# A transformer block in one core: two more tiles by seven products, and part of the low halves on GpSimd

## The chip, the core and the metric

The kernel runs on one core of a Trainium2 chip. The time is the device time of one execution, in microseconds, as the median of several runs. Five engines matter: TensorE (PE in the profile) for matrix products, with its weight loads shown apart (PEld), VectorE (DVE), ScalarE (ACT), GpSimd (POOL), and SyncE (SP), which here only issues transfers.

## The reference: what is computed

One layer of an encoder on 256 tokens of width 2048, all in float32. The first half is an RMS norm, a combined input projection, windowed attention beside a Fourier mix, and an output projection added to x. The second half, where most of the time and most of the change lie, is a feed-forward block with a gate of 5504 channels (43 tiles of 128):

```python
def _conv_ffn(h, w_up, dw_w, dw_b, w_down):
    up = h @ w_up
    gate, val = up[..., :D_FF], up[..., D_FF:]
    gate = conv_width_3(gate, dw_w) + dw_b      # depthwise, along the tokens
    act = jax.nn.gelu(gate, approximate=False) * val
    return act @ w_down

x = x + jnp.concatenate([a, f], axis=-1) @ w_out
x = x + _conv_ffn(_rmsnorm(x, norm2_g), w_up, dw_w, dw_b, w_down)
return _rmsnorm(x, normf_g)
```

(The convolution is written short here.)

## The kernel before: tiles, stages and order

**Split products.** TensorE multiplies in a rounded float32 format (fp32r). To keep accuracy, each weight tile is split into a high part, its rounding, which ScalarE makes (`split_high`, L190, with its operation at L197), and a low part, the rest, which VectorE makes by a subtraction (`split_low`, L199, at L205). Activations are split in the same way, and a product is the sum of three: high by high, high by low, low by high. A weight tile comes as a *unit* of 128 x 2048 values (1 MB) into one of three `raw` buffers by a load on SP's queue; `split(i)` makes the two parts in three rotating buffers each, and once the low part is made, `load(i + 3)` is issued into the raw buffer that came free.

**Feed-forward.** Up units, one for the gate and one for the value of each of the 43 tiles, are still weights: 16 blocks of 128 x 128, each with a matmul of 512 columns for the high part and one of 256 for the low part (L372). Behind them come small steps: `scaled_sum` (L1011) adds the two halves of the sum (ScalarE copies one out, L1013; VectorE adds, L1015) and multiplies by `r2b`, the row of 1/rms (L1016); `gate_conv` (L1019) is the convolution, one operation of ScalarE and two of VectorE; `gate_gelu`; `val_mult`.

**Down projection by seven products.** For most tiles, the down projection works on 2 x 2 blocks: two halves of a group's tiles, two halves of the tokens, and pairs of 512 output columns. Instead of eight block products there are seven, of sums of blocks (a scheme of the Strassen kind). `GROUPS` (L81) names the groups: (first tile, tiles per half). In the kernel before these are tiles 0 to 35: a group of 2 + 2 and four of 4 + 4. Each group is multiplied for two values of c (pairs of columns), so 14 products, named P1, P7, N5, N3, P6, P2, N4. A product with n tiles per half takes 3n matmuls of 512 columns. Its weights are read from a ring of two buffers `rawd` (`ring_load`, on SP's queue) and from `sumw`, a running sum of weight blocks: `first_sums` (L1140) makes the first sum on VectorE, the others are accumulating transfers issued by GpSimd (L1134, L1136, L1145). `split_product` (L1117) splits them (L1129, L1130). The operands are sums of activation blocks, made by `operand` and `operand_sums`. When the last value tile of a group is ready, these steps are spread over the next seven items (`up_posts`).

**The rest.** Tiles in `LATE` (36 to 39) are multiplied directly, as four "down" units of 2048 columns (L355 to L357); tiles in `LAST` (40 to 42) as four "last" units at the very end (L1410 to L1412). Each result is added to x by VectorE (`product_out`, `shared_out`, `down_out`, `last_post`). `first_squares` to `scaled` are the final norm.

**Order.** Nothing is scheduled automatically: each engine runs its instructions in the order in which the program emits them. `ff_items` (L101) writes out the order of the feed-forward: `PATTERNS` (L89) says for each group how up units (u), products (s) and down units (d) follow each other, `"uuu" + "su" * 13 + "s"` for the first four. In step n the matmuls of item n are emitted, then the posts put `beside` it, then the split of item n + 2, then the posts put `behind` it (`ff_step`, L1160). So a split is emitted two items ahead of its matmuls.

**Before the feed-forward**, the output projection works through 16 units with `unit(i, work)`: its matmuls, the steps put beside, the split of unit i + 2, the steps put behind. For each of four column blocks of x, `flip_x_out` turns the block (a transposition on VectorE and four transfers on SP's queue), `flip_x_in` reads it back. For the last block, `last_out_post` (L1298) does that by hand among the first up units, and makes `r2b`: the sum of squares, a power on GpSimd (L309), and a way out to memory and back as a row (`row_out`, L320; `row_in`).

Of the kernel before, what the change touches and what calls it, by code (L numbers as in the profile page):

```python
# [11 lines left out]
ALU = mybir.AluOpType  # L12
# [65 lines left out]
OUT_ORDER += [(c, k) for c in (2, 3) for k in range(4)]  # L78


GROUPS = [(0, 2), (4, 4), (12, 4), (20, 4), (28, 4)]  # L81
LATE = list(range(36, 40))
LAST = list(range(40, NF))
PRODUCTS = [
    ["P1", "P7", "N5", "N3", "P6", "P2", "N4"], ["P1", "N5", "P7", "N3", "P6", "P2", "N4"]
# [1 line left out]


PATTERNS = ["uuu" + "su" * 13 + "s"] * (len(GROUPS) - 1)  # L89
PATTERNS += ["uuu" + "su" * 6 + "sdu" + "ssu" * 2 + "suuss" + "ddd"]  # L90


def group_of(j):
# [7 lines left out]
def ff_items():  # L101


    def ups(first, end):
        return [(kind, j) for j in range(first, end) for kind in ("gate", "val")]

    firsts = [first for first, _ in GROUPS] + [LATE[0], NF]
    items = ups(0, firsts[1])
    for g, pattern in enumerate(PATTERNS):
        todo = {  # L110
            "u": ups(firsts[g + 1], firsts[g + 2]),
            "s": [("product", g, c, p) for c in range(2) for p in PRODUCTS[c]],
            "d": [("down", c) for c in range(4)],
        }
# [6 lines left out]
def block_kernel(  # L121
# [39 lines left out]
    for n, it in enumerate(items):  # L161
        if it[0] == "product":
            continue
        up_index[n] = len(units)
        if it[0] in ("gate", "val"):
            units.append((w_up[2 * it[1] + (it[0] == "val")], 2048))
            shifts.append((0, SHIFT))
            continue
        elif it[0] == "down":
            units.append((w_down_late[it[1]], 2048))  # L170
        else:
            units.append((w_down_last[it[1]], 512 * len(LAST)))
        shifts.append((0, 0))
# [22 lines left out]
        s = slice(o, min(o + n, units[i][1]))  # L196
        nc.scalar.activation(halves[i][0][:, s], raws[i][:, s], AF.Copy)  # L197

    def split_low(i, o=0, n=2048, reload=True):  # L199

        if i >= len(units):
            return
        hi, lo = halves[i]
        s = slice(o, min(o + n, units[i][1]))
        nc.vector.tensor_tensor(lo[:, s], raws[i][:, s], f32(hi[:, s]), ALU.subtract)  # L205
        if s.stop == units[i][1] and reload:
            load(i + RAW)
            load_more(i + RAW)

    def split(i):  # L210

        split_high(i)
        split_low(i)


    pa = ctx.enter_context(ExitStack())
# [739 lines left out]
    for n, (c, kq) in enumerate(OUT_ORDER):  # L956
        i = N_OUT + n

        def work(hi, lo):
            if kq == 0:  # L960
                ps_a[c] = [bank(mm, f"ps_a{c}{b}") for b in range(2)]
            if kq == 3:
                ps_a[c, "f"] = [bank(dn, f"ps_ff{c}{b}") for b in range(2)]
            ps = ps_a[c] if kq < 3 else ps_a[c, "f"]
            for b in range(2):
                moving_weights(
                    hi, lo, 512, range(4 * kq, 4 * kq + 4), cat.get, b, ps[b],
                    kq in (0, 3), kq in (2, 3),
                )

        unit(i, work)
        if kq >= 2:
            part = "a" if kq == 2 else "f"
            ps = ps_a[c] if kq < 3 else ps_a[c, "f"]
            last = c in added
            added.add(c)
            if n == len(OUT_ORDER) - 1:
                last_out = c, part, ps
                continue

            at(behind if (c, kq) == (0, 2) else beside, i + 1, out_add, c, part, ps)
            if last:
                at(behind, i + 1, out_sums, c)
                at(behind, i + 1, flip_x_out, c)
                at(beside, i + 2, flip_x_in, c)
                at(beside, i + 4, flip_x_parts, c)
    pa.close()
# [3 lines left out]
    fp = ctx.enter_context(tc.tile_pool(name="fp", bufs=2))  # L991
    hT[:] = hT2
    r2b = fp.tile([P, S], F32, tag="r2b", name="r2b", bufs=1)
    parts = {}
    gate_out, sums_of, act = {}, {}, {}

# [14 lines left out]
    def scaled_sum(ps, name):  # L1011
        tmp = fp.tile([P, S], F32, tag="ftmp", name=f"ft_{name}")
        nc.scalar.activation(tmp, ps[:, S : 2 * S], AF.Copy)  # L1013
        add = fp.tile([P, S], F32, tag="fadd", name=f"fa_{name}", bufs=3)
        nc.vector.tensor_tensor(add, ps[:, 0:S], tmp, ALU.add)  # L1015
        nc.vector.tensor_tensor(add, add, r2b, ALU.mult)  # L1016
        sums_of[name] = add

    def gate_conv(j):  # L1019
# [94 lines left out]

    pending = []

    def split_product(g, c, p):  # L1117
# [11 lines left out]
        nc.scalar.activation(hi, src, AF.Copy)  # L1129
        nc.vector.tensor_tensor(lo, src, f32(hi), ALU.subtract)  # L1130
        if p in ("P1", "P7", "N3", "P2"):
            ring_load()
        elif p == "N5":
            nc.gpsimd.dma_start(x, weights_of(g, c, "d"), accum_op=ALU.add)  # L1134
# [12 lines left out]
    def split_item(n):  # L1147
        if n >= len(items):
            return
        it = items[n]  # L1150
        if n in up_index:
            split(up_index[n])
            if pending:
                pending.pop(0)()
        else:
            while pending:
                pending.pop(0)()
            split_product(*it[1:])

    def ff_step(n):  # L1160
        run(beside, n)
# [34 lines left out]
    def product_out(g, c, p, ps):  # L1196
# [7 lines left out]
        else:  # L1204
            n, t = {"P2": (0, 0), "N3": (1, 0), "N4": (0, 1)}[p]
            xb = xs[2 * n + c][:, t, :]
            tt(xb, ps, xb, ALU.add)

    def shared_out(c, step):

# [8 lines left out]
        elif step == 1:  # L1219
            tt(u, u, p7, ALU.add)  # L1220
            tt(x01, x01, st["w", c], ALU.add)
            tt(x10, x10, u, ALU.add)
        else:
            w = st.pop(("w", c))
            tt(w, w, p7, ALU.subtract)
            tt(x11, x11, w, ALU.add)

    def by_parts(ps, o, hi, lo, n, first, last):

# [12 lines left out]
    ssq3 = base.tile([P, 2, 32], F32, tag="ssq3", name="ssq3")  # L1242

    def first_squares(b):
        nc.vector.tensor_scalar(ssq3[:, b, 3:4], ssq3[:, b, 0:1], EPS, None, ALU.add)

    ready = {(c, b): xs[c][:, b, :] for c in range(4) for b in range(2)}

# [49 lines left out]
    def last_out_post(c, part, ps):  # L1298
# [10 lines left out]
        nc.vector.tensor_reduce(tot2, ssq2, mybir.AxisListType.X, ALU.add)  # L1309
        rstd_of(tot2, D, "2", r=r2b[:, 0:2])  # L1310
        split_low(i, 1024, 1024, reload=False)
        row = row_out(r2b, "2")
        flip_x_in(c)
        row_in(row, r2b)
        load(i + RAW)
# [36 lines left out]
    for n, it in enumerate(items):  # L1352
        if n < OPEN:
            continue
        if it[0] == "last":
            break
        if n in (4, 5):
            ring_load()
        if n == 6:
            pending.append(lambda: first_sums(0, 0))  # L1360
        if it[0] in ("gate", "val"):
            kind, j = it
# [199 lines left out]
```

## Time and profile before

| | |
|---|---|
| Runs before | 933.44, 933.64, 950.5 us; median 933.64 |
| Profiled execution | 933.83 us; span from first to last instruction 932.1 us; granted clock 0.998 |
| TensorE busy | 923.2 us, 4973 matmuls |
| VectorE busy | 776.2 us, 997 instructions |
| ScalarE busy | 543.6 us |
| GpSimd busy | 62.8 us |
| Read from memory | 216.98 MB |

How to read it: the profile is one execution. "Busy" is the time in which an engine had an instruction running; a matmul's shown length (0.39 us for 512 columns) overlaps with the next one, so that the pace is read from the starts. A row of the groups names the line, the engine, the operation, what it writes and reads with the shapes, the count, the busy time and the mean length in ns, and then the idle time ahead of these instructions with what ended it. A row of the timeline has the start, the length, and the same names. A row of the windows has a stretch, its length, and the busy time of each engine with its number of instructions.

### The profile page before, as it was taken

The numbers are of one execution on the slowest core, as the hardware profiler recorded it, in microseconds if no ns is written. First come the engines' busy times: TensorE is split into PE (matmuls) and PEld (weight loads), VectorE is DVE, ScalarE is ACT, GpSimd is POOL, SyncE is SP. The second block draws the span as 40 slices with busy tenths as digits, with TensorE's granted clock in tenths as the row PEclk, the third lists the DMA queues.
The fourth block names the chain that finished last, engine by engine and source line by source line (L and its number), as shares of the span: only waits on it lengthen the run. The fifth ranks groups of instructions, "written<-read, shape, count | busy, mean of one in ns | idle before, by whom it ended". The sixth has DMA issues, their size and how long they took to land.

```text
span 932.1 us, 12883 instructions
## 1 busy us (share of the span) xinstructions
PE 923.2 (99%) x4973; PEld 799.9 (86%) x4973; DVE 776.2 (83%) x997; ACT 543.6 (58%) x689; POOL 62.8 (7%) x79
## 2 busy tenths in 40 slices
PE   9999999999999999999999999999999999999996
PEld 7888998888888888888888888888888888888885
DVE  7768998787768877898877997888978789989995
ACT  6756777546465655565555665555755556655553
POOL 0101111200000000000000000000000000000002
PEclk9999999999999999999999999999999999999999
DMA  9865777667777668788797769887787968779652
GB/s 361 331 225 158 249 241 215 201 198 269 230 274 256 203 207 256 242 274 263 229 299 251 240 209 298 223 260 233 268 240 244 306 221 269 237 238 272 203 180 91
DMA packets 59597, 225.16 MB, mean 242 GB/s; under 512 B 24465, under 2 KB 30225, under 8 KB 35984
## 3 DMA queue, kind: packets, MB, share of 16 engines
q1 hardware_dynamic: 54928, 194.72, 57.9%
q0 software_dynamic: 4464, 29.36, 17.0%
q8 instruction: 39, 0.64, 0.3%
q10 hardware_dynamic: 144, 0.26, 0.1%
q14 instruction: 22, 0.18, 0.0%
HBM read 216.98 MB, written 7.08 MB: 240 GB/s over the span
## 4 chain that ended last, share of the span: by engine, by line
PE 98%; DMA 0%; ACT 0%; DVE 0%; issue 0%; POOLq 0%; POOL 0%; ACTq 0%
PE ps_gate L372 25%; PE ps_val L372 25%; PE ps_q L372 7%; PE ps_P L1233 4%; PE ps_P L1234 4%; PE ps_P L1232 3%; PE ps_N L1233 3%; PE ps_N L1234 3%; PE ps_N L1232 3%; PE ps_k L372 2%; PE ps_a L357 2%; PE ps_a L355 2%; PE ps_a L356 2%; PE ps_s L748 1%; PE ps_o L842 1%; PE ps_ff L355 1%
## 5 line engine op out<-in xcount | busy, mean ns | idle before, releaser
L205 DVE TENSOR_TENSOR lo<-raw,hi 128x2048 fp32r<-128x2048 f32 (+2 forms) x133 | 295.0, 2221 | 28.3 <-ACT hi L197 28.0
L197 ACT ACTIVATE hi<-raw 128x2048 fp32r<-128x2048 f32 (+1 forms) x131 | 246.8, 1887 | 27.6 <-PE ps_a L356 10.8
L372 PE MATMUL ps_gate<-hU,hi 128*128 128x512 f32 x688 | 236.1, 389 | 0.0
L372 PE MATMUL ps_val<-hU,hi 128*128 128x512 f32 x688 | 236.1, 389 | 0.0
L372 PE MATMUL ps_gate<-hU,lo 128*128 128x256 f32 x688 | 189.9, 276 | 0.0
L372 PE MATMUL ps_val<-hU,lo 128*128 128x256 f32 x687 | 189.6, 276 | 0.0
L372 PEld LDWEIGHTS ps_gate<-hU,hi 128*128 128x128 f32 x688 | 129.2, 188 | 26.8
L372 PEld LDWEIGHTS ps_val<-hU,hi 128*128 128x128 f32 x688 | 129.2, 188 | 26.8
L372 PEld LDWEIGHTS ps_gate<-hU,lo 128*128 128x128 f32 x688 | 129.2, 188 | 1.3
L372 PEld LDWEIGHTS ps_val<-hU,lo 128*128 128x128 f32 x687 | 129.0, 188 | 1.3
L1013 ACT ACTIVATE ft_g<-ps_gate 128x256 f32<-128x256 f32 x43 | 16.5, 384 | 121.1 <-PE ps_gate L372 121.1
L1013 ACT ACTIVATE ft_v<-ps_val 128x256 f32<-128x256 f32 x43 | 16.5, 383 | 87.0 <-PE ps_val L372 87.0
L372 PE MATMUL ps_q<-hT,hi 128*128 128x512 f32 x192 | 65.0, 391 | 0.0
L1232 PE MATMUL ps_P<-hi_P,op_P 128*128 128x512 f32 x144 | 56.0, 389 | 0.0
L1233 PE MATMUL ps_P<-hi_P,op_P 128*128 128x512 f32 x144 | 56.0, 389 | 0.0
L1234 PE MATMUL ps_P<-lo_P,op_P 128*128 128x512 f32 x144 | 56.0, 389 | 0.0
L372 PE MATMUL ps_q<-hT,lo 128*128 128x256 f32 x192 | 51.2, 277 | 0.0
L1130 DVE TENSOR_TENSOR lo_N<-sumw,hi_N 128x2048 fp32r<-128x2048 f32 (+1 forms) x20 | 41.5, 2076 | 9.4 <-ACT hi_N L1129 9.2
L1232 PE MATMUL ps_N<-hi_N,op_N 128*128 128x512 f32 x108 | 42.0, 389 | 0.0
L1233 PE MATMUL ps_N<-hi_N,op_N 128*128 128x512 f32 x108 | 42.0, 389 | 0.0
L1234 PE MATMUL ps_N<-lo_N,op_N 128*128 128x512 f32 x108 | 42.0, 389 | 0.0
L372 PEld LDWEIGHTS ps_q<-hT,hi 128*128 128x128 f32 x192 | 35.2, 188 | 6.6
(415 smaller groups left out, 1592.4 us busy)
## 6 DMA issues: line engine op xcount, KB each, us to landing
raw<-in_w_up SPq DMA_DIRECT2D x86, 1024.0 KB, 6.6
raw<-in_w_in SPq DMA_DIRECT2D x20, 1024.0 KB, 5.4
raw<-in_w_out SPq DMA_DIRECT2D x16, 1024.0 KB, 5.1
sumw<-in_w_down POOLq DMA_DIRECT2D x16, 1024.0 KB, 8.6
raw<-in_w_down_late SPq DMA_DIRECT2D x4, 1024.0 KB, 6.8
raw<-in_w_down_last SPq DMA_DIRECT2D x4, 768.0 KB, 4.0
turnp<-flip SPq DMA_DIRECT2D x44, 64.0 KB, 1.9
flop<-turnp SPq DMA_DIRECT2D x11, 256.0 KB, 3.9
```

What stands on the lines that cost most here:

```text
L197: nc.scalar.activation(halves[i][0][:, s], raws[i][:, s], AF.Copy)
L205: nc.vector.tensor_tensor(lo[:, s], raws[i][:, s], f32(hi[:, s]), ALU.subtract)
L355: nc.tensor.matmul(ps, ah, wh, start=first and q == q0, stop=False)
L356: nc.tensor.matmul(ps, al, wh, start=False, stop=False)
L357: nc.tensor.matmul(ps, ah, wl, start=False, stop=last and q == q0 + len(kk) - 1)
L372: nc.tensor.matmul(ps[:, x], (hi, lo)[i][:, k * P : (k + 1) * P], hk(k)[:, x], start=n == 0 and k == 0, stop=n == len(order) - 1 and k == ...
L748: nc.tensor.matmul(ps[:, b * S : (b + 1) * S], qT[:, qo + b * P : qo + (b + 1) * P], kT[:, ko : ko + S], start=n == 0, stop=n == 2,)
L1013: nc.scalar.activation(tmp, ps[:, S : 2 * S], AF.Copy)
L1130: nc.vector.tensor_tensor(lo, src, f32(hi), ALU.subtract)
L1232: nc.tensor.matmul(ps, o[:, 0, p, :], hi[:, s], start=first and p == 0, stop=False)
L1233: nc.tensor.matmul(ps, o[:, 1, p, :], hi[:, s], start=False, stop=False)
L1234: nc.tensor.matmul(ps, o[:, 0, p, :], lo[:, s], start=False, stop=last and p == n - 1)
```

## The change

- `GROUPS` and `LATE`: group 0 has 3 + 3 tiles instead of 2 + 2, all groups begin two tiles later, so 38 tiles go by seven products; the late units are tiles 38 and 39 only, 1024 columns each.
- `low_part`: for items from 12 on (all products, and all up units behind the first twelve), a low part of 2048 columns is made in two: VectorE makes 1408 columns, GpSimd 640. Narrower ones stay on VectorE.
- The order of the last group is written anew, with the down units in the order 0, 2, 1, 3.
- The value is no longer multiplied by `r2b`. Instead, x is multiplied by rms (`rms2`) where the first group's results are added to it, and the final norm's epsilon by rms squared (`eps3`): the result is the same, as that norm divides out a factor per token.
- `flip_x_out` is put ahead of the split for column blocks other than the first.
- The first ring loads and the first sum move four items later, with the first product.

```diff
-GROUPS = [(0, 2), (4, 4), (12, 4), (20, 4), (28, 4)]
-LATE = list(range(36, 40))
+GROUPS = [(0, 3), (6, 4), (14, 4), (22, 4), (30, 4)]
+LATE = list(range(38, 40))
...
-PATTERNS += ["uuu" + "su" * 6 + "sdu" + "ssu" * 2 + "suuss" + "ddd"]
+PATTERNS += ["uuu" + "sss" + "usususus" + "dssussdsususdd"]
+DOWN_ORDER = [0, 2, 1, 3]
+SHARE = 640
+SHARE_FROM = 12
...
-            "d": [("down", c) for c in range(4)],
+            "d": [("down", c) for c in DOWN_ORDER],
...
-            units.append((w_down_late[it[1]], 2048))
+            units.append((w_down_late[it[1]], 512 * len(LATE)))
...
+    def low_part(lo, src, hi, shared):
+
+        n = lo.shape[1]
+        m = n - n // 2048 * SHARE * shared
+        nc.vector.tensor_tensor(lo[:, 0:m], src[:, 0:m], f32(hi[:, 0:m]), ALU.subtract)
+        if m < n:
+            nc.gpsimd.tensor_tensor(lo[:, m:n], src[:, m:n], f32(hi[:, m:n]), ALU.subtract)
...
-        nc.vector.tensor_tensor(lo[:, s], raws[i][:, s], f32(hi[:, s]), ALU.subtract)
+        low_part(lo[:, s], raws[i][:, s], hi[:, s], shared)
...
-                at(behind, i + 1, flip_x_out, c)
+                at(beside if c else behind, i + 1, flip_x_out, c)
...
-        nc.vector.tensor_tensor(add, add, r2b, ALU.mult)
+        if name[0] == "g":
+            nc.vector.tensor_tensor(add, add, r2b, ALU.mult)
...
-        nc.vector.tensor_tensor(lo, src, f32(hi), ALU.subtract)
+        low_part(lo, src, hi, shared)
...
-            split(up_index[n])
+            split(up_index[n], n >= SHARE_FROM)
...
-            split_product(*it[1:])
+            split_product(*it[1:], n >= SHARE_FROM)
...
-            tt(xb, ps, xb, ALU.add)
+            if g == 0:
+                nc.vector.scalar_tensor_tensor(xb, xb, rms2[:, t : t + 1], ps, ALU.mult, ALU.add)
+            else:
+                tt(xb, ps, xb, ALU.add)
...
-            tt(x11, x11, w, ALU.add)
+            nc.vector.scalar_tensor_tensor(x11, x11, rms2[:, 1:2], w, ALU.mult, ALU.add)
...
-        nc.vector.tensor_scalar(ssq3[:, b, 3:4], ssq3[:, b, 0:1], EPS, None, ALU.add)
+        nc.vector.tensor_scalar(
+            ssq3[:, b, 3:4], ssq3[:, b, 0:1], eps3[:, b : b + 1], None, ALU.add
+        )
...
+        nc.vector.reciprocal(rms2, r2b[:, 0:2])
         row = row_out(r2b, "2")
+        nc.vector.tensor_tensor(eps3, rms2, rms2, ALU.mult)
+        nc.vector.tensor_scalar(eps3, eps3, EPS, None, ALU.mult)
...
-        if n in (4, 5):
+        if n in (8, 9):
             ring_load()
-        if n == 6:
+        if n == 10:
             pending.append(lambda: first_sums(0, 0))
```

More of the change, by code (lines that the diff above doesn't have):

```diff
@@ L197, in split_high, with split_low @@
         nc.scalar.activation(halves[i][0][:, s], raws[i][:, s], AF.Copy)
-    def split_low(i, o=0, n=2048, reload=True):
+    def low_part(lo, src, hi, shared):
[4 more added lines that the diff above has]
+            nc.gpsimd.tensor_tensor(lo[:, m:n], src[:, m:n], f32(hi[:, m:n]), ALU.subtract)
+    def split_low(i, o=0, n=2048, reload=True, shared=False):
         if i >= len(units):
@@ L208, in split_low, with split @@
             load_more(i + RAW)
-    def split(i):
+    def split(i, shared=False):
         split_high(i)
-        split_low(i)
+        split_low(i, shared=shared)
     pa = ctx.enter_context(ExitStack())
@@ L993, in block_kernel @@
     r2b = fp.tile([P, S], F32, tag="r2b", name="r2b", bufs=1)
+    rms2, eps3 = vcol(V_N + NH, 2), vcol(V_N + NH + 2, 2)
     parts = {}
@@ L1115, in block_kernel, with split_product @@
     pending = []
-    def split_product(g, c, p):
+    def split_product(g, c, p, shared):
         raw = {w: ring_tiles.get((g, c, w)) for w in "abcd"}
```

## The prediction

> **What bounds the kernel now.** I read the page first (shares, slices, chain), then stretches of the feed-forward by windows, then one period of it in the timeline.
>
> ```profile
> span 932.1 us, 12883 instructions
> ...
> PE 923.2 (99%) x4973; PEld 799.9 (86%) x4973; DVE 776.2 (83%) x997; ACT 543.6 (58%) x689; POOL 62.8 (7%) x79
> ...
> PE 98%; DMA 0%; ACT 0%; DVE 0%; issue 0%; POOLq 0%; POOL 0%; ACTq 0%
> ```
>
> The profiled execution took 933.83 us (span 932.1 and 1.7 around it), the median of the runs shown is 933.64, so I sum against 933.83. TensorE is the chain. The next three rows are one whole group of the feed-forward, the last stretch (from the first tile after group 3 to the last four units), and the end.
>
> ```profile
> core 0: us, PE busy (x) PEld busy (x) DVE busy (x) ACT busy (x) POOL busy (x), PEclk, DMA share, GB/s
> ...
> 540.66:665.80 125.14, 125.14 (x681) 108.72 (x681) 107.11 (x110) 72.18 (x71) 5.26 (x6) 1.00 0.81 252
> 771.69:907.76 136.07, 136.07 (x713) 117.01 (x712) 124.48 (x135) 77.37 (x76) 5.83 (x7) 1.00 0.76 237
> 907.76:932.10 24.34, 16.60 (x82) 13.93 (x80) 13.65 (x26) 9.39 (x20) 5.58 (x8) 0.91 0.23 87
> ```
>
> TensorE never pauses there; VectorE (DVE) fills 86% and 91% of the two stretches, so it is next in line. The chain of waits gives the rate of TensorE.
>
> ```profile
> 548.82 5.44 PE ps_gate L372 x32
> ...
> 581.46 5.44 PE ps_gate L372 x32
> 589.62 5.44 PE ps_val L372 x32
> ```
>
> An up unit is 5.44 us. Between 581.46 and 589.62 lie one up unit and one product of 12 matmuls, so those are 2.72 us, 0.227 us each, and a pair is 8.16. One such pair, on ScalarE and VectorE:
>
> ```profile
> 572.84 2.29 DVE L1130 TENSOR_TENSOR lo_P<-rawd20c,hi_P 128x2048 fp32r<-128x2048 f32 x1 [0.92 <-ACT hi_P L1129]
> 573.19 1.91 ACT L197 ACTIVATE hi<-raw 128x2048 fp32r<-128x2048 f32 x1
> 575.04 0.48 DVE L1024 SCALAR_TENSOR_TENSOR cv<-fa_g,vec,cv 128x255 f32<-128x255 f32 x1
> ...
> 575.96 0.68 DVE L1203 TENSOR_TENSOR z_P<-ps_P,z_P 128x512 f32<-128x512 f32 x1
> ...
> 576.56 2.28 DVE L205 TENSOR_TENSOR lo<-raw,hi 128x2048 fp32r<-128x2048 f32 x1
> ```
>
> The low part that ends at 578.84 is read by the up unit at 581.46: a lead of 2.6 us. It is smallest where a group's operands are made:
>
> ```profile
> 541.07 1.91 ACT L197 ACTIVATE hi<-raw 128x2048 fp32r<-128x2048 f32 x1
> ...
> 545.25 2.28 DVE L205 TENSOR_TENSOR lo<-raw,hi 128x2048 fp32r<-128x2048 f32 x1
> ```
>
> It ends at 547.53 and is read at 548.82: 1.3 us.
>
> **TensorE's part of the change.** Tiles 36 and 37 go from direct products to group 0. Direct, two tiles cost 4 column blocks x 2 token blocks x 3 x 2 = 48 matmuls; by seven products 2 x 7 x 3 = 42. Six fewer: 6 x 0.227 = **-1.36 us**, all on the path. Nothing else shortens it, as no pauses exist to be removed.
>
> **VectorE's part.** Durations by kind:
>
> ```profile
> L205 DVE TENSOR_TENSOR lo<-raw,hi 128x2048 fp32r<-128x2048 f32 x122 | 278.9, 2286 | 27.1 <-ACT hi L197 26.8
> ...
> L1016 DVE TENSOR_TENSOR fa_v<-fa_v,r2b 128x256 f32<-128x256 f32 x43 | 18.3, 425 | 1.5
> L1015 DVE TENSOR_TENSOR fa_v<-ps_val,ft_v 128x256 f32<-128x256 f32 x43 | 18.2, 422 | 17.0 <-ACT ft_v L1013 17.0
> ...
> L205 DVE TENSOR_TENSOR lo<-raw,hi 128x1024 fp32r<-128x1024 f32 x4 | 4.8, 1221 | 0.1
> ```
>
> (2286 - 1221)/1024 = 1.04 ns a column, so 640 columns fewer save 0.664 us a unit. 74 up units (items from 12 on) and 56 products of groups 1 to 4 are shared: 130 units, 86 us. The value's factor goes: 43 x 0.425 = 18 us. Group 0's wider products and narrower late units add 14 x 512 - 4 x 1024 = 3072 columns, 3 us. The eight multiply-adds with `rms2` replace adds of one size, one for one: nothing.
>
> **GpSimd's part.** Its nearest rows:
>
> ```profile
> L1134 POOL DMA_DIRECT2D sumw<-in_w_down x8 | 7.0, 876 | 155.0 <-DVE lo_N L1130 155.0
> ...
> L1253 POOL TENSOR_TENSOR xs<-xs,gfb 128x512 f32<-128x512 f32 x3 | 3.9, 1293 | 26.8 <-ACT junkc L1262 26.8
> ...
> L554 POOL TENSOR_TENSOR sq_f<-sq_f,sq 128x256 f32<-128x256 f32 x3 | 2.2, 745 | 5.2 <-ACT sq L550 5.2
> ```
>
> (1293 - 745)/256 = 2.14 ns a column; 640 columns make 1293 + 128 x 2.14 = 1.57 us. In a group that is 47 of 125 us, with six DMA issues of 0.88: GpSimd itself has room. The question is what it does to VectorE. One place shows both at once:
>
> ```profile
> 173.66 2.29 DVE L205 TENSOR_TENSOR lo<-raw,hi 128x2048 fp32r<-128x2048 f32 x1
> ...
> 174.74 1.81 POOL L554 TENSOR_TENSOR sq_a<-sq_a,sq 128x256 f32<-128x256 f32 x1 [3.44 <-ACT sq L550]
> ...
> 175.86 1.30 DVE L833 TENSOR_TENSOR pt<-flop,pt 128x256 fp32r<-128x256 f32 x2
> ```
>
> ```profile
> 128.11 0.75 DVE L833 TENSOR_TENSOR pt<-flop,pt 128x256 fp32r<-128x256 f32 x2
> ```
>
> GpSimd takes 1.81 us for what takes 0.745 alone: it stands until the low part ends. Then VectorE's pair, also with both inputs in SBUF, takes 1.30 instead of 0.75: it stands 0.55 behind GpSimd. They exclude each other. For 640 columns the block on VectorE is 0.55 + 384 x 2.14 ns = 1.37 us (the mean row would make it 1.57 at most). A VectorE operation with one input in PSUM is not held:
>
> ```profile
> 910.94 0.68 DVE L1258 TENSOR_TENSOR xs<-ps_e,xs 128x512 f32<-128x512 f32 x1
> ...
> 912.46 1.29 POOL L1253 TENSOR_TENSOR xs<-xs,gfb 128x512 f32<-128x512 f32 x1 [26.23 <-ACT junkc L1262]
> 912.49 0.69 DVE L1258 TENSOR_TENSOR xs<-ps_e,xs 128x512 f32<-128x512 f32 x1
> ```
>
> So sharing takes 0.664 us from VectorE and puts 1.37 in its way, unless an operation of the second kind, or idleness, lies beside.
>
> [...]
>
> *A full group* (patterns 1 to 3, 30 shared units): VectorE 107.1 - 30 x 0.664 - 8 x 0.425 = 83.8; blocks 30 x 1.37 = 41.1; together 124.9 of 125.1 if nothing is covered. 16 adds of 0.422 and 10 product adds of 0.68 can lie beside: 13.6 us. So the group as a whole fits, and what is lost is lost locally, at its change, where the operands of the finished group are made between the splits:
>
> ```profile
> 518.92:547.53 28.61, 27.41 (x33) 1.00 0.79 258
> ```
>
> In these 28.61 us VectorE is busy 27.41, so 1.2 are idle, and it makes six low parts. Each is now 1.37 - 0.664 = 0.71 us worse: 4.2. The pair before hands on 2 x 0.71 = 1.4 (its idleness, 0.92 in the row at 572.84, comes ahead of the low part and cannot take it up). Two value factors go: 0.85. So the unit read at 548.82 comes 1.4 + 4.2 - 0.85 - 1.2 - 1.3 (lead) = 2.3 us late if nothing is covered. The stretch holds four adds of 0.422 and one of 0.68, 2.4 us, which would cover it all. ScalarE gives no help: the high part at 541.07 stands behind a convolution that waits for VectorE. I take the middle, 1.15, as I see cover and no cover about equally often in the order of the operations: **3 x 1.15 = 3.5 us** (ends 0 and 6.9). Pattern 0 has its 14 products unshared and only half the blocks: 0.
>
> In mid-group, the sum for the next column block:
>
> ```profile
> 586.34 2.29 DVE L1144 TENSOR_TENSOR sumw<-rawd21a,rawd21b 128x2048 f32<-128x2048 f32 x1
> ...
> 589.16 0.88 POOL L1145 DMA_DIRECT2D rawd21b<-in_w_down  x1 [21.02 <-ACT hi_P L1129]
> ```
>
> This accumulating DMA waits in GpSimd's queue for the sum, and the next low parts stand behind it to 590.0. They are read 5 us later; I take 0 (up to 0.4 each).
>
> *Last stretch.* TensorE: 136.07 less 4 up units (21.76) and 4 x 2.72 of late products = 103.4. VectorE: 124.5, less 4 up units with their posts (4 x (2.286 + 0.422 + 0.425) and 2 x (0.96 + 0.84) = 16.1), 4 x 1.065 for the late units, 24 x 0.664 and 5 x 0.425: 86.0. Blocks 24 x 1.37 = 32.9. Together 118.9 against 103.4 + 2.6 of lead = 106.0: 12.9 too much with no cover. 10 adds (4.2) and 20 of 0.68 on PSUM (6 products, 6 shared sums, 8 late) are 17.9 us of possible cover: 5.0 to spare. Middle **+4.0 us** (ends 0 and 12.9). The first place to suffer is "sss" after the tile change: P1, P7 and N5 follow each other in 2.7 us steps, and the operand of N5 is made only behind the split of N5, which follows two low parts and two blocks.
>
> *Edits with small prices.* `rms2` puts a 128x2 reciprocal ahead of the transposition of `r2b`:
>
> ```profile
> 254.33 0.21 DVE L322 STREAM_TRANSPOSE r2b<-r2b 128x32 f32<-128x32 f32 x1 [0.60 <-POOL r2b L309]
> ```
>
> About that size, 0.2 us on the row's way out and so, on SP's queue, on the load of the last x block behind it; both end ahead of the opening's last products by some tenths: between 0 and 0.2, I take 0. The two `eps3` operations delay a low part by as much, also hidden. `flip_x_out` before the split for two blocks delays a low part by one transposition; it is for a unit two places on, 2 x 24 x 0.227 = 10.9 us of products, which cover it; SP's four small transfers move ahead of one weight load with three buffers: 0. Raw buffers now wait for GpSimd too, at worst 1.6 us later than now, with three units of 8 us a pair to land in: 0. The late blocks' order 0, 2, 1, 3 moves bank use alone. The first two loads of the ring (768 KB now, not 512), the first sum and its accumulating DMA are issued four items later, as their products are: the distances stay, so 0. Behind the last product nothing changes but an operand of `first_squares`: 0.
>
> Sum: 933.83 - 1.36 + 3.5 + 4.0 = **940.0 us**.
>
> **Rivals.** *Covered:* every block falls beside adds or idleness; then 933.83 - 1.36 = 932.5. For it: 13.6 and 17.9 us of adds against 0 and 12.9 needed. Against it: both engines start on the same event, the end of the high part, and the operation after a low part is mostly a convolution or product with two SBUF inputs.
> *VectorE becomes the bound (the other side):* with no cover and the whole 1.57 us as block, a group needs 83.8 + 47.1 = 130.9 of 125.1 and the last stretch 86.0 + 37.7 = 123.7 of 106.0: 3 x 5.8 + 17.7 - 1.36 = +33.7, **967.6**. It passes 2% from a block b with 3 x (83.8 + 30b - 125.1) + 24b + 86.0 - 106.0 = 20.0, that is 1.44 us uncovered. For it: 1.37 is near, from one event. Against: TensorE's delay itself gives VectorE time.
> [...]
>
> **How the numbers follow.** Partly covered (forecast, own range 934 to 951): 0.47. Covered (931.5 to 934): 0.35. VectorE the bound (951 and up): 0.17. Below 931.5: 0.01. The range 931.5 to 954 leaves out 0.01 below and about 0.13 above. 2% (18.7 us) is about what a measurement of this kernel can tell from no change: faster 0.01, within 0.84, slower 0.15.
>
> **What would show it.** 4967 matmuls; DVE low parts of 128x1408 near 1.62 us where free and 2.9 to 3.1 where they stood behind GpSimd; POOL about 200 us busier; convolutions above 0.48; pauses of TensorE only at the group changes and in the last 120 us, waiting for `lo`. If 128x1408 and the convolutions keep their length, exclusion is wrong and the time is 932.5. If TensorE pauses evenly in every pair, VectorE is the bound. A pause before 300 us would make the small prices wrong.

## The result, and the profile after

Six executions of the changed kernel took 962.07 to 970.02 us, median 965.22; the kernel before, beside it, 933.59. The ratio is 1.035 (95% interval 1.032 to 1.038): slower by 3.5%. The prediction was 940.0 us with a range to 954. (Some executions of before, and of the kernels below in which GpSimd does not read, are about 16 us longer than the rest, and the ratios leave these out.)

The profiled execution took 965.19 us, 31.4 more than that of before. First the page: the span, the busy times and the chain that ended last.

```profile
span 963.4 us, 13166 instructions
...
PE 937.4 (97%) x4967; PEld 802.7 (83%) x4967; DVE 831.1 (86%) x955; ACT 546.9 (57%) x687; POOL 351.5 (36%) x209
...
PE 74%; DVE 18%; issue 4%; ACT 2%; DMA 1%; POOL 0%; POOLq 0%; DVEq 0%; ACTq 0%
```

TensorE has its 4967 matmuls, but is 26 us short of the span, where before it was 9. VectorE holds 18% of the chain instead of 0. It was to lose about 86 us of low parts and 18 of factors; instead its busy time rose by 55. The windows of a full group and of the last stretch (from 28 us ahead of the last group's N5 to the last up unit) show where:

```profile
core 0: us, PE busy (x) PEld busy (x) DVE busy (x) ACT busy (x) POOL busy (x), PEclk, DMA share, GB/s
...
545.00:670.00 125.00, 122.27 (x664) 105.26 (x663) 117.15 (x100) 69.52 (x67) 71.93 (x36) 1.00 0.79 248
...
814.00:928.20 114.20, 105.89 (x531) 88.52 (x530) 110.36 (x101) 59.83 (x58) 53.91 (x31) 0.97 0.71 203
```

VectorE is 94% and 97% busy there, though no operation was added. The groups of VectorE in the first of these windows, by form (columns: count, busy time, mean ns of one, idle time before):

```profile
L208 DVE TENSOR_TENSOR lo<-raw,hi 128x1408 fp32r<-128x1408 f32 x16 | 31.4, 1960 | 0.0
L1039 DVE SCALAR_TENSOR_TENSOR cv<-fa_g,vec,cv 128x255 f32<-128x255 f32 x8 | 11.8, 1477 | 0.0
L1068 DVE TENSOR_TENSOR va3k<-fa_v,cv 128x256 f32<-128x256 f32 x6 | 11.6, 1929 | 0.0
L1042 DVE SCALAR_TENSOR_TENSOR cv<-fa_g,vec,cv 128x255 f32<-128x255 f32 x8 | 7.4, 930 | 0.3
L208 DVE TENSOR_TENSOR lo_N<-sumw,hi_N 128x1408 fp32r<-128x1408 f32 x4 | 6.5, 1626 | 1.9 <-ACT hi_N L1144 1.7
...
L1029 DVE TENSOR_TENSOR fa_g<-ps_gate,ft_g 128x256 f32<-128x256 f32 x8 | 3.3, 416 | 0.8 <-ACT ft_g L1027 0.6
```

A low part of 1408 columns takes 1.63 us where it is free, as predicted. The convolution at L1039, 0.48 us before, takes 1.48; the product with the value (L1068) takes 1.93. The add at L1029 reads one input from PSUM and keeps its 0.42. GpSimd's side, over the whole run:

```profile
L210 POOL TENSOR_TENSOR lo<-raw,hi 128x640 fp32r<-128x640 f32 x74 | 151.9, 2054 | 140.2 <-ACT hi L202 128.1 <-DVE cv L1042 8.4 <-DVE cv L1039 3.6
L210 POOL TENSOR_TENSOR lo_N<-sumw,hi_N 128x640 fp32r<-128x640 f32 x16 | 45.7, 2855 | 57.7 <-ACT hi_N L1144 57.7
```

It starts when ScalarE's high part ends. Where VectorE starts its low part at that moment too, GpSimd stands behind it (2.86 us); else it takes mostly 1.6 to 1.9. So the two exclude each other, as the prediction said. What that does to the path is seen in the timeline at a group's change (start, length, engine; [idle time <- what ended it]):

```profile
579.92 1.82 POOL L210 TENSOR_TENSOR lo_P<-rawd20b,hi_P 128x640 fp32r<-128x640 f32 x1 [3.48 <-ACT hi_P L1144]
580.24 1.79 DVE L1068 TENSOR_TENSOR va3k<-fa_v,cv 128x256 f32<-128x256 f32 x1
...
581.95 0.41 DVE L1029 TENSOR_TENSOR fa_g<-ps_gate,ft_g 128x256 f32<-128x256 f32 x1
...
582.74 1.62 DVE L208 TENSOR_TENSOR lo_P<-rawd20b,hi_P 128x1408 fp32r<-128x1408 f32 x1
582.86 0.60 ACT L1038 ACTIVATE cv<-fa_g,vec 128x256 f32<-128x256 f32 x1 [2.50 <-DVE fa_g L1031]
583.37 1.90 ACT L202 ACTIVATE hi<-raw 128x2048 fp32r<-128x2048 f32 x1
...
585.00 0.69 DVE L1108 TENSOR_TENSOR va2k<-va2k,va2k 128x512 f32<-128x512 f32 x1
585.35 1.77 POOL L210 TENSOR_TENSOR lo<-raw,hi 128x640 fp32r<-128x640 f32 x1 [3.61 <-ACT hi L202]
585.61 2.06 DVE L1097 TENSOR_TENSOR op_N<-va2k,op_N 128x512 fp32r<-128x512 f32 x1
...
588.06 0.39 PE L385 MATMUL ps_gate<-hU,hi 128*128 128x512 f32 x1
...
588.50 1.62 DVE L208 TENSOR_TENSOR lo<-raw,hi 128x1408 fp32r<-128x1408 f32 x1
...
590.17 0.39 PE L385 MATMUL ps_gate<-hU,lo 128*128 128x256 f32 x1 [1.72 <-DVE lo L208]
```

VectorE's queue is full here, so it isn't at its low part when the high part ends. GpSimd starts as soon as the operation in hand is done (its 1.82 and 1.77 us are 0.25 and 0.20 above the shortest from 545 to 670 us, 1.57), ahead of VectorE's next one, and that one waits for nearly all of GpSimd's work: `va3k` 1.79 us instead of 0.42, `op_N` 2.06 instead of 0.69. Both times this is 1.37 us more, the uncovered block that the prediction had worked out. Each lengthens the queue ahead of VectorE's own, later part of the same low part. ScalarE's queue passes it on: its convolution stood 2.50 us and the next high part behind it. The low part that TensorE wanted at 588.3 ends at 590.1, and TensorE pauses 1.88 us (counted from the starts of the matmuls; the row shows 1.72 of idleness). The longest pause is the operand of N5 in the new "sss":

```profile
840.80 1.61 DVE L208 TENSOR_TENSOR lo_N<-sumw,hi_N 128x1408 fp32r<-128x1408 f32 x1
...
843.05 0.69 DVE L1108 TENSOR_TENSOR va4k<-va4k,va4k 128x512 f32<-128x512 f32 x1
843.58 1.84 POOL L210 TENSOR_TENSOR lo<-raw,hi 128x640 fp32r<-128x640 f32 x1
843.66 2.32 DVE L1097 TENSOR_TENSOR op_N<-va4k,op_N 128x512 fp32r<-128x512 f32 x1
846.03 0.79 PE L1251 MATMUL ps_N<-hi_N,op_N 128*128 128x512 f32 x1 [3.71 <-DVE op_N L1097]
```

From the starts of all matmuls, set against the pace of before, the time adds up as follows. Pauses: 8.6 us in the groups (1.4, 3.1 and 3.2 at the three changes, 0.8 in mid-group) and 10.5 in the last stretch (3.9 at N5, 6.7 behind it). 2.7 us in 13 matmuls at half the clock behind the pause at N5 (starts 0.43 apart). 9.4 us of a slower pace. 1.8 us more behind the last matmul. Less 1.36 for the matmuls and 0.2 in the opening: 31.4, and the spans differ by 31.3.

Behind the opening, every wait of TensorE in the profile's list ends with a result of VectorE, and none with one of GpSimd. The three largest (engine, line, what it waited for: us in total, times, longest):

```profile
PE ps_gate L385 <- DVE lo L208: 6.1, 4, 2.5
PE ps_val L385 <- DVE lo L208: 4.3, 4, 1.8
PE ps_N L1251 <- DVE op_N L1097: 3.7, 1, 3.7
```

### The profile page after: what moved, and what is told of

It is laid out like the page before. It is cut to its first block, busy times and chain, and to the rows that moved or that the text cites. A ratio compares the mean times of both kernels' runs of the same rounds, so it can differ in the third digit from the quotient of the medians.

```text
span 963.4 us, 13166 instructions
## 1 busy us (share of the span) xinstructions
PE 937.4 (97%) x4967; PEld 802.7 (83%) x4967; DVE 831.1 (86%) x955; ACT 546.9 (57%) x687; POOL 351.5 (36%) x209
## 4 chain that ended last, share of the span: by engine, by line
PE 74%; DVE 18%; issue 4%; ACT 2%; DMA 1%; POOL 0%; POOLq 0%; DVEq 0%; ACTq 0%
PE ps_gate L385 18%; PE ps_val L385 18%; PE ps_q L385 7%; DVE lo L208 3%; PE ps_k L385 2%; PE ps_a L368 2%; PE ps_a L370 2%; PE ps_a L369 2%; PE ps_P L1250 2%; PE ps_P L1252 2%; PE ps_P L1251 2%; DVE lo_P L208 2%; PE ps_N L1251 2%; PE ps_N L1252 2%; DVE cv L1039 2%
## 5 line engine op out<-in xcount | busy, mean ns | idle before, releaser
L208 DVE TENSOR_TENSOR lo<-raw,hi 128x1408 fp32r<-128x1408 f32 (+3 forms) x133 | 275.0, 2070 | 29.4 <-ACT hi L202 28.9
L202 ACT ACTIVATE hi<-raw 128x2048 fp32r<-128x2048 f32 (+2 forms) x131 | 243.4, 1861 | 30.7 <-PE ps_a L369 12.4
L385 PE MATMUL ps_gate<-hU,hi 128*128 128x512 f32 x688 | 240.5, 393 | 0.0
L385 PE MATMUL ps_val<-hU,hi 128*128 128x512 f32 x688 | 240.1, 393 | 0.0
L210 POOL TENSOR_TENSOR lo<-raw,hi 128x640 fp32r<-128x640 f32 x74 | 151.9, 2054 | 140.2 <-ACT hi L202 128.1
L210 POOL TENSOR_TENSOR lo_N<-sumw,hi_N 128x640 fp32r<-128x640 f32 x16 | 45.7, 2855 | 57.7 <-ACT hi_N L1144 57.7
L1251 PE MATMUL ps_P<-hi_P,op_P 128*128 128x512 f32 x152 | 59.4, 391 | 0.0
L1250 PE MATMUL ps_P<-hi_P,op_P 128*128 128x512 f32 x152 | 59.1, 389 | 0.0
L1049 ACT ACTIVATE cv<-cv 128x256 f32<-128x256 f32 x43 | 17.9, 417 | 67.7 <-DVE cv L1042 67.3
L1251 PE MATMUL ps_N<-hi_N,op_N 128*128 128x512 f32 x114 | 45.6, 400 | 3.7 <-DVE op_N L1097 3.7
L1039 DVE SCALAR_TENSOR_TENSOR cv<-fa_g,vec,cv 128x255 f32<-128x255 f32 x43 | 48.5, 1127 | 0.4 <-ACT cv L1038 0.4
```

What stands on the lines that cost most here:

```text
L208: nc.vector.tensor_tensor(lo[:, 0:m], src[:, 0:m], f32(hi[:, 0:m]), ALU.subtract)
L210: nc.gpsimd.tensor_tensor(lo[:, m:n], src[:, m:n], f32(hi[:, m:n]), ALU.subtract)
L385: nc.tensor.matmul(ps[:, x], (hi, lo)[i][:, k * P : (k + 1) * P], hk(k)[:, x], start=n == 0 and k == 0, stop=n == len(order) - 1 and k == ...
L1039: nc.vector.scalar_tensor_tensor(cv[:, 1:S], ga[:, 0 : S - 1], w[0], cv[:, 1:S], ALU.mult, ALU.add)
L1049: nc.scalar.activation(cv, cv, AF.Gelu)
L1250: nc.tensor.matmul(ps, o[:, 0, p, :], hi[:, s], start=first and p == 0, stop=False)
```

## Experiments

The theory: GpSimd's reading and VectorE's operations with two inputs in SBUF exclude each other, and what this delays is VectorE's queue; all of the loss behind the first GpSimd low part is that. Rivals: the regrouping and the new last stretch cost time by themselves (A); it is the late arrival of GpSimd's 640 columns, not what it does to VectorE (B); the small edits have a price (C).

**e1: no sharing.** `SHARE = 0`, all else of the change.

> The changed kernel with SHARE = 0: VectorE makes every low part whole, all else as changed. Theory T1 (GpSimd's part and VectorE's operations with two SBUF inputs exclude each other, and this makes VectorE late): all pauses go, 932.5 us (931.5 to 934). Rival R1 (the new order of the last stretch costs by itself): the pauses behind 840 us stay, 945 to 950. Rival R3 (TensorE's slower pace in some stretches comes from GpSimd's work): the pace is 0.340 us per pair of matmuls throughout; if the pace has another cause, up to 8 us remain on top.

Measured: 939.08 us, ratio 1.0055 (1.0040 to 1.0069). No pause in the groups; those left are in the last stretch, 1.03 us at N5, 0.62 and 1.83 at low parts, 0.31 in the last units. Windows of e1, a group and the last stretch (the same work as 814.00:928.20 above):

```profile
545.00:670.00 125.00, 125.00 (x681) 108.45 (x680) 103.65 (x102) 71.89 (x70) 5.24 (x6) 1.00 0.81 253
...
796.20:902.20 106.00, 103.00 (x535) 87.51 (x534) 97.86 (x103) 59.42 (x59) 5.81 (x7) 1.00 0.75 223
```

So sharing causes every pause in the groups, and A holds in part: without any sharing the time is 5.4 us above that of before, though 1.36 us of matmuls are saved. Neither expected time was met: not all pauses go, but those that stay are small.

**e2: sharing alone.** The kernel before, with `low_part` from item 8 on, and nothing else of the change.

> The kernel before with nothing but the shared low parts (from item 8 on): old groups, old order of the last stretch, value still scaled. T1: VectorE is late at the three group changes (about 2.5 us each) and in the last stretch, where 124.5 - 32 x 0.664 + 32 x 1.37 = 147 stand against 136.1 + 2.6: 933.6 + 7.5 + 8 = 949 (942 to 958). R1: only the group changes, about 941. R2 (only the result of GpSimd is late, VectorE is not disturbed): 934, as the old leads are 2.6 us.

Measured: 958.42 us, ratio 1.0261 (1.0246 to 1.0275). 17.6 us of pauses over 0.25 us, mostly in pairs around each change and in mid-group, and two stretches at half the granted clock behind pauses of 2.3 and 2.6 us; with small delays, pauses and clock make 22.3 us. So sharing by itself makes this kernel slower. The loss is larger than I expected; that VectorE still carries the value's factor here (0.425 us a pair), and so has less room, may be why, but no run tests it.

**e3: GpSimd reads, and nobody waits for it.** VectorE makes every low part whole; GpSimd makes a difference of 512 columns into a scratch tile, in items 12 to 131.

```diff
-        nc.vector.tensor_tensor(lo[:, 0:m], src[:, 0:m], f32(hi[:, 0:m]), ALU.subtract)
+        nc.vector.tensor_tensor(lo, src, f32(hi), ALU.subtract)
         if m < n:
-            nc.gpsimd.tensor_tensor(lo[:, m:n], src[:, m:n], f32(hi[:, m:n]), ALU.subtract)
+            side = wp.tile([P, 512], F32, tag="junk", name="side")
+            nc.gpsimd.tensor_tensor(side, src[:, 0:512], f32(hi[:, 0:512]), ALU.subtract)
```

> VectorE makes every low part whole; GpSimd, in the same places up to the last group, subtracts 512 columns of the same tiles into a scratch tile that nobody reads. T1: a block of 0.55 + 256 x 2.14 ns = 1.10 us a unit on top of the whole low part: a group needs 83.8 + 30 x 0.664 + 33 = 136.7 of 125.1, so 3 x 11.6 = 35 us lost: 967 (958 to 976), convolutions and value products on VectorE far above 0.48 and 0.42 us. R2 (lateness of GpSimd's result): nobody waits for it, 932.5. R1: as e1.

Measured: 974.46 us, ratio 1.0424 (1.0407 to 1.0442). VectorE's groups of e3 in the same window:

```profile
L208 DVE TENSOR_TENSOR lo<-raw,hi 128x2048 fp32r<-128x2048 f32 x15 | 38.0, 2532 | 0.0
L208 DVE TENSOR_TENSOR lo_N<-sumw,hi_N 128x2048 fp32r<-128x2048 f32 x4 | 12.7, 3178 | 0.0
L1040 DVE SCALAR_TENSOR_TENSOR cv<-fa_g,vec,cv 128x255 f32<-128x255 f32 x7 | 8.5, 1215 | 0.0
```

Nothing waits for a result of GpSimd, and it costs more than the change does. B is out as the cause, as the waits of the changed kernel said: the price is paid by VectorE.

**e4: GpSimd writes.** As e3, but GpSimd reads 8 columns and then writes 512 columns three times (`memset`).

> As e3, but GpSimd reads only 8 columns of the high part (so that it starts at the same moment) and then writes 512 columns of scratch three times by memset. T1 in its narrow form (GpSimd's reads exclude VectorE's second input): about as e1, 932.5 to 936. T1 in a wide form (any SBUF access of GpSimd excludes it): VectorE's two-input operations are lengthened as in e3 and the time is above 950.

Measured: ratio 1.0060 (1.0041 to 1.0079), two executions at 939.37 and 939.39 us: those of e1. GpSimd is as long at work, and VectorE doesn't feel it (groups of e4 on VectorE, the same window):

```profile
L208 DVE TENSOR_TENSOR lo<-raw,hi 128x2048 fp32r<-128x2048 f32 x16 | 36.5, 2283 | 0.6 <-ACT hi L202 0.6
...
L1042 DVE SCALAR_TENSOR_TENSOR cv<-fa_g,vec,cv 128x255 f32<-128x255 f32 x8 | 3.8, 479 | 0.0
```

So it is GpSimd's reading alone that holds VectorE up: its first operation of the convolution takes 479 ns beside the writing, against 1215 beside the reading of e3 and 477 in e1.

**e5 and e6: sharing in the last group only, and in the groups only.** `SHARE_FROM = 132`; and `12 <= n < 132`.

> The changed kernel with SHARE_FROM = 132: GpSimd shares only in the last group. T1 (exclusion, place by place): no pause before 800 us; behind it the pauses of the changed kernel's last stretch (about 13 us with the slow clock after the longest). 932.5 + 13 + 1 for the end = 946 (943 to 950). If the losses of the groups only move along the chain (a rival: one backlog that is carried on), the last stretch alone would lose less than 13, and e5 and e6 would not add up to the changed kernel.

> The changed kernel with sharing only in items 12 to 131, not in the last group. T1: the pauses of the three group changes and mid-groups as in the changed kernel (about 8 us), then the last stretch of e1 (4 to 5): 945 (942 to 953; the upper end is for stretches of slower pace of TensorE). A rival by which GpSimd's work itself slows TensorE's clock: stretches of 0.350 instead of 0.340 us per pair of matmuls before 800 us, as in the changed kernel, and none behind.

Measured: e5 949.41 us, ratio 1.0193 (1.0148 to 1.0238), three executions at 948.1 to 950.5 and the profiled one at 961.6, with 16.9 us of the slower pace; less these it would be at 944.7. The others' larger time fits their clock, whose mean is lower (0.992 to 0.994 against 0.996): the profiled execution has no half clock behind its pause at N5. e6 950.42 us, ratio 1.0184 (1.0169 to 1.0198). Against e1, sharing in the groups costs 11.3 us and in the last group some 9 (948.2 against 939.1). Both together would make about 959.7; the changed kernel has 965.2 and, in e10, 961.8. I had expected 946 and 945: both are dearer than thought, though inside their ranges.

**e7 and e11: the last stretch in other orders**, without sharing. The last pattern is `"uuu" + "ssussususus" + "dsussdssususdd"` in e7 and `"uuu" + "sussusususs" + "dsussdssususdd"` with the shared sums two items apart in e11.

> SHARE = 0 and another order of the last group: uuu ssussususus d su s s d s s u s u s d d in place of uuu sss usususus d ss u ss d s u s u s d d, so that up units stand between the products where e1 pauses. Theory (in e1 the remaining loss is VectorE being late behind runs of short products): the pauses of 1.7 and 1.8 us go, 933 to 936. Rival (VectorE's sum in the last stretch, about 102 of 103.4 us, is too much in any order): the pauses only move, 937 to 940.

> No sharing, all else of the change, and the last group's products spread once more: the pattern is uuu, sussusususs, dsussdssususdd, with the shared sums two items apart. Theory (VectorE's work in the last stretch, about 102 of 103.4 us, is too much in any order): pauses of 2 to 5 us in the last 120 us, only moved; 937 to 940 us. Rival (the order of e1 and e7 was to blame): pauses under 1.5 us in all, 932.5 to 935 us, which would beat the kernel before by 0 to 1 us.

Measured: ratios 1.0050 (1.0036 to 1.0065) and 1.0055 (1.0041 to 1.0069); the executions compared are at 938.4 to 939.4 and 937.3 to 940.8 us. Neither clearly beats e1's 939.1, and both stay above the kernel before. In e7 the pauses only move (0.97, 0.49, 0.65, 0.79 and 0.65 us). The longest one of e1 comes from bunching: five result adds stand ahead of the low part that TensorE wants, of which the last and what follows are

```profile
868.86 0.68 DVE L1257 TENSOR_TENSOR xs<-ps_N,xs 128x512 f32<-128x512 f32 x1
869.46 2.28 DVE L208 TENSOR_TENSOR lo<-raw,hi 128x2048 fp32r<-128x2048 f32 x1
...
869.73 0.40 PE L385 MATMUL ps_val<-hU,hi 128*128 128x512 f32 x1
...
871.79 0.38 PE L385 MATMUL ps_val<-hU,lo 128*128 128x256 f32 x1 [1.67 <-DVE lo L208]
```

**e8: 256 columns.** `SHARE = 256`.

> The changed kernel with GpSimd making 256 columns instead of 640. T1: a unit costs VectorE 0.55 of block less 0.27 saved, 0.28 instead of 0.71 us, so at a group change 2 x 0.28 + 6 x 0.28 - 0.85 - 1.2 - 1.3 is below zero: no pause in the groups; the last stretch loses e1's 4 us and up to 24 x 0.28 = 7 more: 940 (937 to 946). Rival (loss by the presence of GpSimd's instructions, whatever their length): pauses at the group changes as in the changed kernel, above 955.

Measured: 941.44 us, ratio 1.0084 (1.0071 to 1.0097); no pause in the groups, 2.54 and 1.90 us in the last stretch, with half the granted clock behind the first. The convolution at L1039 takes 844 ns instead of 1477 in the group's window. The loss follows the size of GpSimd's part, and at 256 columns the lead takes up everything in the groups, as the expectation's sum had it; where between 256 and 640 the pauses begin, no run shows.

**e9: the small edits alone.** The changed kernel with the old `GROUPS`, `LATE`, last pattern and ring times, and `SHARE = 0`.

> The changed kernel with the old GROUPS, LATE, last pattern, ring times and no sharing: what is left of the change are the dropped value factor, rms2, eps3 and the transposition ahead of the split (the small prices that the prediction put at 0). Theory (they cost nothing, the loss of e1 comes from the regrouped last stretch alone): 933.6 us (933.2 to 934.3), no pause of TensorE, 4973 matmuls. Rival (part of e1's 5.4 us is theirs): 935 to 939 us, with a pause ahead of 300 us or in mid-group.

Measured: 934.06 us, ratio 1.0001 (0.9992 to 1.0011), no pause of TensorE behind the opening. `rms2`, `eps3`, the dropped factor and the earlier transposition cost nothing, and C is out.

**e10: the changed kernel once more.**

> The changed kernel as it is, a second profiled execution. Theory (the pauses are the program's, the slower pace of TensorE at a granted clock of 1.00 is the execution's): 962 to 970 us; pauses at the same places with the same lengths within 0.1 us, 22 us in all; up pairs of 0.350 instead of 0.340 us in other stretches than 256 to 512 and 768 to 856, so that the pace's share differs from 9.6 us by more than 2. Rival (the pace belongs to the program, as a result of sharing): the same stretches and 9.6 us within 1.

Measured: 960.91 us in the profiled execution, 961.77 in the median of two. 21.2 us of pauses and of half clock behind N5, at the same places except for some of 0.3 us. I had expected the same lengths, and not all are: at N5 5.1 us instead of 3.9, at the three changes 1.7, 3.0 and 1.3 instead of 1.2, 2.9 and 2.9 (waits over 0.25 us alone). The slower pace is 5.6 us instead of 9.6 and lies elsewhere, mainly from 592 to 768 us instead of from 256 to 512 and from 768 to 856. Where it holds, the pauses are the shorter ones (the first change of the first profile, the third of e10): there the slower TensorE waited less. TensorE's timeline of the first profile at 300 us:

```profile
299.89 0.40 PE L385 MATMUL ps_val<-hU,hi 128*128 128x512 f32 x1
...
300.24 0.40 PE L385 MATMUL ps_val<-hU,hi 128*128 128x512 f32 x1
```

and of e10, at 300 and at 640 us:

```profile
299.75 0.39 PE L385 MATMUL ps_val<-hU,hi 128*128 128x512 f32 x1
...
300.09 0.39 PE L385 MATMUL ps_val<-hU,hi 128*128 128x512 f32 x1
...
639.68 0.40 PE L385 MATMUL ps_gate<-hU,hi 128*128 128x512 f32 x1
...
640.03 0.40 PE L385 MATMUL ps_gate<-hU,hi 128*128 128x512 f32 x1
```

From one high-part matmul to the next is 0.35, 0.34 and 0.35 us, all at a granted clock shown as 1.00. So the place and length of this pace belong to the execution, not to the program.

**e12: sharing without reading.** GpSimd writes zeros into its 640 columns instead of the difference, so that these columns of the low parts are left out of the products; VectorE's low parts are as short as in the change.

```diff
-            nc.gpsimd.tensor_tensor(lo[:, m:n], src[:, m:n], f32(hi[:, m:n]), ALU.subtract)
+            nc.gpsimd.memset(f32(lo[:, m:n]), 0.0)
```

> The changed kernel, but GpSimd writes zeros into its 640 columns of each low part and reads nothing: these columns of the low parts are left out of the products. VectorE has the shorter low parts of the change (1408 columns, 0.664 us less each), TensorE the same matmuls, GpSimd the same number of instructions. Theory (all of the loss is GpSimd's reading beside VectorE, and the new last stretch loses only as VectorE's sum there is too large): 932.5 us (931.5 to 933.5), no pause over 0.3 us, convolutions at 0.48, up pairs at 0.340. Rival A (the order of the last stretch is late whatever VectorE has to do): 934 to 938, with the pause at N5 still there. Rival B (a second writer of the low part's buffer holds TensorE or the loads): 936 to 960, with pauses in the groups.

Measured: 935.99 us, ratio 1.0022 (1.0013 to 1.0031). Windows of e12, the same two stretches of work, and the one place that is still late:

```profile
545.00:670.00 125.00, 125.00 (x681) 108.64 (x680) 84.42 (x101) 71.75 (x70) 24.21 (x36) 1.00 0.80 251
...
797.40:900.20 102.80, 102.53 (x535) 87.45 (x534) 82.35 (x101) 59.19 (x59) 20.30 (x30) 1.00 0.79 233
```

```profile
826.05 0.50 PE L1251 MATMUL ps_N<-hi_N,op_N 128*128 128x512 f32 x1 [0.27 <-DVE op_N L1097]
```

The one edit is that GpSimd doesn't read, which also makes its work shorter (24 us in the first window against 72): 29 us. That its mere presence at work is not the cause is what e4 shows. No pause is left in the groups. In the last stretch, e1's three pauses before the last units shrink to one of 0.4 us at N5, with 20 us of VectorE's time to spare: so most of the regrouping's pauses, and about half of its whole loss (6.6 us above 932.5 in e1, 3.5 here), come from VectorE's load. A remainder (rival A of its expectation, 934 to 938) stays with the new order. Of the 3.7 us between 932.5 and the 936.1 of the profiled execution, 1.1 are pauses, 1.4 small delays (0.6 at the feed-forward's start, and in the last 70 us some 0.8 of the slower pace of e10) and 1.2 lie behind the start of the last matmul, where VectorE comes later to the final norm: 9.14 us (934.35 less 925.21) against 7.98 (932.06 less 924.08) before.

## Why the prediction was wrong

*The mechanism* (GpSimd and VectorE exclude each other for two SBUF inputs; an operation with PSUM is not held; the loss is local) was right: e3, e4 and e12 show the exclusion (1215, 479 and 478 ns for VectorE's first operation of the convolution), the add at L1029 with one input in PSUM keeps its 0.42 us in the changed kernel, and the places of the pauses, in e5 and e6 too, show that the loss is local. The two terms that carry the sum were too small by more than half. The loss that the new order has by itself was missed, and TensorE's slower pace stands in no step.

*TensorE's -1.36 us:* right, 4967 matmuls.

*VectorE's sum:* right. A group without blocks was to need 83.8 us: e12 has 84.42. With blocks, 117.15 of 122.27 us of TensorE's time is 119.8 in 125.0; less 84.4 and over 30 shared parts that is 1.18 us a block, against the predicted 1.37 uncovered and 0.92 with all 13.6 us of cover. In the last stretch 110.36 less 82.35 over 24 is 1.17. So, if a block is 1.37 us, as `va3k` and `op_N` show it, cover is some 6 us a group, not 13.6, and VectorE as a whole still fits, as was said.

*Group changes, "I take the middle, 1.15, as I see cover and no cover about equally often": this step failed.* The block was right and its cover was not. The three measured 1.4, 3.1 and 3.2 us, 7.7 in place of 3.5, the last two above the uncovered 2.3. Both engines were taken to start on the same event, the end of the high part, so that VectorE's low part would go first and adds beside GpSimd would cover the rest. At a change VectorE is behind: it is in some other operation when the high part ends, GpSimd goes ahead of its queue, and the block falls in front of the low part that TensorE waits for, on operands and convolutions. The add that was to cover it comes too late for that: in the change shown, the next one starts at 581.95 us, when GpSimd's work of 579.92 has just ended. The second pause, one item later (1.0 us), was not in the sum at all. *Mid-group,* taken as 0 with up to 0.4 each: 0.8 in two places.

*Last stretch, "Middle +4.0 us (ends 0 and 12.9)": failed in the same way and in two more.* Pauses and the half clock make 13.2 us, near the uncovered end as a number, but that is in part luck, as 4.3 of them are not sharing's. The place, N5 in "sss", was named. The middle of the ends 0 and 12.9 would have been 6.4; 4.0 is the middle of 12.9 and a surplus of 5.0, which no time can be gained from. And missed was that the new order loses 4.3 us of pauses with no sharing at all (e1): the sum over the stretch, VectorE 97.9 of 106 us, said that it fits, but five adds of 0.68 us ahead of one low part do not ask the sum. With sharing left out of the stretch, the prediction's way of counting would have given 932.5.

*Behind the last product, "nothing changes":* 1.8 us later, 1.1 and 1.2 in e1 and e12, as VectorE arrives late at the final norm.

*Small prices at 0:* right (e9).

*The rivals.* "Covered" is out. "VectorE becomes the bound" gave 967.6, near the measured 965.2, but not by its working: blocks were 1.18 us, below its threshold of 1.44, VectorE still idles in places, and TensorE pauses at changes and not in every pair. It is the forecast's mechanism at its uncovered ends, plus 9.4 us of slower pace. GpSimd's queue is out as a cause as well: no wait of TensorE ends with GpSimd's part, and e3 loses more where nobody waits for it.

*Open:* why TensorE's pace falls by 2 to 3% in stretches. It was in both profiles of the changed kernel (9.4 to 9.6 us by the way of counting, and 5.6) and in those of e2, e3, e5 and e6. Those of e1, e4, e7, e8 and e12 have under 1 us of it, behind 820 us, and that of e9 has none. But it lies elsewhere in each execution, and the profiled execution of e11 (954.12 us, no sharing) has it from the feed-forward's start on. In the groups it sets in at the feed-forward's start or at a unit in which TensorE has just waited for its low part (at 769.48 us in the first profile of the changed kernel, at 593.74 in e10), and the unshared profiles have no such waits there. So sharing may bring it on by its pauses; no run tests that.

## What to carry to other kernels

Moving work with two SBUF inputs from a nearly full VectorE to GpSimd did not pay here: each 640 columns took 0.66 us off VectorE and put 1.18 back, and only writing went beside it free (its first operation of the convolution 479 and 478 ns in e4 and e12, against 477 in e1). Where an engine is nearly full (86 to 97% in the stretches here), look not at its sum over a stretch but at the longest run of operations in its queue between an input's arrival and the result that TensorE waits for; that run, with every block placed in it, was the delay here. And a helper that starts on an early event went ahead of a queue that was late, so its cost fell in the very places where there was no slack (1.37 us each on `va3k` and `op_N` at a group's change).

## What the runs showed of the hardware that was not expected

- GpSimd, which waits for an operation of VectorE to end, goes ahead of VectorE's next one even where that follows at once (the rows from 579.92 and 585.35 us, where the next ones take 1.79 and 2.06 us instead of 0.42 and 0.69). So it is mostly not the other part of the same low part that is held (in the group's window 23 of VectorE's 29 take 1.61 to 1.63 us, and six 2.4 to 3.6) but what stands ahead of it (the convolution 1.48 instead of 0.48).
- Writing alone by GpSimd, 167 us of it in e4, costs VectorE nothing that can be measured: in the group's window the low parts take 2283 ns (2284 in e1) and its two operations of the convolution 479 and 485 (477 and 485).
- Behind the pause of 3.9 us, 13 matmuls ran at a granted clock of 0.50:

```profile
846.00:849.00 3.00, 2.96 (x7) 2.39 (x8) 2.96 (x5) 1.67 (x2) 0.00 (x0) 0.50 1.05 218
```

  The length of the pause does not decide it. At the same place, e8 idles 2.38 us and has the half clock behind it, and e5 idles 3.55 us and has none (first the two rows of e8, then those of e5):

```profile
827.12 0.79 PE L1251 MATMUL ps_N<-hi_N,op_N 128*128 128x512 f32 x1 [2.38 <-DVE op_N L1097]
827.00:830.00 3.00, 2.88 (x7) 2.31 (x8) 2.96 (x5) 1.72 (x3) 0.00 (x0) 0.50 0.98 202
...
844.21 0.50 PE L1251 MATMUL ps_N<-hi_N,op_N 128*128 128x512 f32 x1 [3.55 <-DVE op_N L1097]
844.00:847.00 3.00, 2.79 (x12) 2.18 (x13) 2.96 (x6) 1.72 (x3) 0.00 (x0) 1.00 1.04 216
```

  The shortest idle time with it was 2.12 us (e2, at 429.19). What decides it stays open here.
- TensorE has two paces, 0.340 and 0.350 us from one high-part matmul of an up unit to the next, at a granted clock of 1.00 in both (the first from 299.75 us of e10, the second from 299.89 us of the first profile and from 639.68 us of e10).
